# Three input chunks accumulated while the features arrive, and the rotation's two products taken from PSUM

## The chip, the cores and the metric

The kernel runs on one core of one Trainium2 chip. The metric is the device time of the core in microseconds (us); the kernel before takes 868.41 us (median of three runs, 867.76 to 868.47). The engines are called PE (matrix products), DVE (vector), ACT (scalar), POOL (GpSimd) and SP (it issues most DMAs). Products accumulate in banks of PSUM; all other tiles lie in SBUF.

## The reference

Two layers of an encoder over 16 meta tokens and 512 real ones, 1024 features, all in float32. Cut to what matters here:

```python
def hybrid_layer(x, norm_g, w_in, q_norm_g, k_norm_g, ...):
    h = rms_norm(x, norm_g)
    proj = einsum('bld,de->ble', h, w_in)
    qa, ka, va, za, qb, kb, vb, zb, ga, gb = split_cols(proj)
    qa = apply_axial_rope(rms_norm(qa.reshape(b, l, 8, 64), q_norm_g), cos, sin)
    ka = apply_axial_rope(rms_norm(ka.reshape(b, l, 2, 64), k_norm_g), cos, sin)
    oa = gqa_attention(qa, ka, va) * silu(za)             # 8 query heads, 2 key heads
    ob = neighbourhood_attention(qb, kb, vb, rpb) * silu(zb)
    mixed = sigmoid(ga) * (oa @ w_o_attn) + sigmoid(gb) * (ob @ w_o_na)
    return x + mixed @ w_out

def apply_axial_rope(x, cos, sin):
    rot = concat([-xr[16:], xr[:16], -xc[16:], xc[:16]])  # xr, xc: the 32 features for row and column
    return x * cos + rot * sin
```

## The kernel before

**Layout.** Features lie on the 128 partitions, tokens along the free axis: 528 tokens, in layer 0 as two spans of 264 (0 and 264), in layer 1 as one of 512. The input projection is made in chunks of 128 output columns: QA to QA+3 (0 to 3, the eight query heads), KA (4), VA (5), then the chunks of the two attentions and the gates. A chunk's span is 24 products into one bank: 8 feature tiles k, and for each the three products wh·hh, wh·hl, wl·hh, since weights and features are split into a high part (hi, cast by ACT) and the rest (lo, subtracted by POOL for weights at L227, by DVE for features at L324). Products go through two banks with the tag "pp" (`product`, L300); the next span takes the bank that the span before last left.

**Norm.** The features enter the products scaled by the gain alone. The squares of the input are made by ACT (L330), added by DVE (L401), split, and averaged by ten tiny products ms (L356). For Q and K each head has its own norm: ACT makes the squares of each chunk twice (qh rounded, qs full), DVE subtracts them to ql (L463), and PE averages them with four products mh for each chunk (L444).

**The head of layer 0.** Ten warming products of two instructions each come first. `piece` loads a quarter of a chunk (two feature tiles' weights), `half` the other half, `feature` a feature tile; `in_order` holds them in the order of the list. QA and QA+1 accumulate while the tiles arrive, QA in the two banks of pp, QA+1 in the two-bank score tile S (one buffer in the whole kernel); their 96 products are written out at L423. QA+2, QA+3, KA, VA follow through `product`.

**Q and K.** `rotated` empties a chunk: ACT reads a bank three times (q times gain L459, squares L460 and L461), after which the bank is free. `rotate` then works in SBUF on DVE: shuffle of q by 16 partitions (L468), times sin (L469), q times cos (L470), their sum (L471). `stack_pair` splits q for the score products (ACT L481, DVE L483) and moves halves by DMA.

**Order.** Every engine runs its instructions in the order that the scheduler put them in when the program was built; `issue_after` holds one behind another in it. The attentions run beside the projections: `product` calls `tick()` behind each span, and the two `Side` objects put their parts (score products S, softmax, transposes pt, value products av) at set numbers of ticks: GQA_AT and NA_AT for the units, NORM_AT for the norms ("tokens" for split, ms and spread; "squares" for mh). S and the one for meta queries, Sm, share the single two-bank buffer, which DVE's L750 empties.

## Time and profile before

| | us |
|---|---|
| median of three runs | 868.41 (867.76 to 868.47) |
| the profiled execution's own time | 869.61 |
| its span, from the first to the last instruction | 867.8 |
| PE busy in the span | 854.8 |
| DVE, ACT, POOL busy in the span | 537.2, 494.2, 365.6 |
| first product of QA+3 / of KA / of VA | 27.70 / 35.34 / 41.75 |

A row of the timeline gives the start, the busy time, the engine, the line and operation, out<-in, shapes, and in brackets how long the engine had stood idle and who released it. A row of the groups gives the count, the busy time, the mean of one in ns and the idle time before. A row of the waits gives who waits for whom, the us in total, how often, and the longest. A row of windows gives, for a stretch, its length and each engine's busy time with its count, the granted clock of PE (1.00 is full speed), the DMA share and GB/s.

### The profile page before, as it was taken

How to read it: one execution, taken by the hardware profiler on the slowest of the kernel's cores; microseconds unless marked ns; L12 is line 12 of the kernel's file. 1: busy time of each engine (PE TensorE's matmuls, PEld its weight loads, DVE VectorE, ACT ScalarE, POOL GpSimd, SP SyncE). 2: the span in 40 equal slices, each digit the busy share in tenths (PEclk: the TensorE clock that was granted, in tenths of full speed). 3: DMA queues.
4: the chain of work that ended last, by engine and by line, in shares of the span. 5: the costliest groups of instructions: out<-in, count | busy, mean ns of one | idle time of the engine just before them, and what ended most of it. 6: DMA issues, size and time to landing. Idle time of an engine off the chain costs nothing.

```text
span 867.8 us, 16234 instructions
## 1 busy us (share of the span) xinstructions
PE 854.8 (99%) x5976; PEld 790.6 (91%) x5976; DVE 537.2 (62%) x1277; ACT 494.2 (57%) x1170; POOL 365.6 (42%) x300
## 2 busy tenths in 40 slices
PE   8999999999999999999999999999999999999997
PEld 8999999999999999999998989898988888888786
DVE  5985667676774574436547656677767646454633
ACT  7645677677774555333445456677767645543432
POOL 5564323443223332544764643334333333334751
PEclk9999999999999999999999999999999999999999
DMA  6364253325112222325555664235422222223602
GB/s 223 99 186 145 93 150 99 106 73 153 49 50 75 62 67 81 98 86 152 148 139 127 171 198 130 79 95 151 145 81 73 86 73 73 87 85 97 206 25 97
DMA packets 64671, 95.76 MB, mean 110 GB/s; under 512 B 22864, under 2 KB 23376, under 8 KB 64592
## 3 DMA queue, kind: packets, MB, share of 16 engines
q1 hardware_dynamic: 63872, 93.66, 36.8%
q8 instruction: 47, 0.77, 0.4%
q10 hardware_dynamic: 720, 1.06, 0.3%
q14 instruction: 32, 0.26, 0.1%
HBM read 76.72 MB, written 4.19 MB: 93 GB/s over the span
## 4 chain that ended last, share of the span: by engine, by line
PE 86%; ACT 6%; DVE 4%; DMA 2%; issue 1%; POOL 0%; SPq 0%; POOLq 0%; ACTq 0%; DVEq 0%
PE pp L311 18%; PE pp L309 18%; PE pp L310 17%; PE y L309 4%; PE y L311 4%; PE y L310 3%; PE av L797 3%; PE pt L124 3%; PE avb L940 2%; PE pf L1115 2%; PE S L525 2%; PE pf L1117 2%; PE pf L1116 1%; PE S L526 1%; DMA x<-in_xT_dram 1%
## 5 line engine op out<-in xcount | busy, mean ns | idle before, releaser
L227 POOL TENSOR_TENSOR wlo<-raw,whi 128x512 fp32r<-128x512 f32 x214 | 285.3, 1337 | 425.4 <-ACT whi L226 341.7
L309 PE MATMUL pp<-hh,whi 128*128 128x264 f32 (+1 forms) x1056 | 334.7, 317 | 0.6 <-ACT qs L461 0.5
L311 PE MATMUL pp<-hh,wlo 128*128 128x264 f32 (+1 forms) x1056 | 329.3, 312 | 0.0
L310 PE MATMUL pp<-hl,whi 128*128 128x264 f32 (+1 forms) x1056 | 328.6, 311 | 0.0
L226 ACT CAST whi<-raw 128x512 fp32r<-128x512 f32 x214 | 131.5, 619 | 152.7 <-PE pp L310 58.3
L311 PEld LDWEIGHTS pp<-hh,wlo 128*128 128x128 f32 x1056 | 198.8, 188 | 10.7
L309 PEld LDWEIGHTS pp<-hh,whi 128*128 128x128 f32 x1056 | 198.6, 188 | 10.1 <-ACT qs L461 1.1
L310 PEld LDWEIGHTS pp<-hl,whi 128*128 128x128 f32 x1056 | 199.3, 189 | 9.0
L750 DVE CUSTOM_DVE_ANT_1 P<-S,r 128x528 f32<-128x528 f32 x64 | 45.1, 704 | 18.5 <-PE S L526 17.6
L183 DVE TENSOR_TENSOR ptl<-pt,pth 128x512 fp32r<-128x512 f32 x64 | 44.0, 689 | 18.0 <-ACT pth L182 17.2
L1012 DVE TENSOR_TENSOR mg<-pp,rbc 128x264 f32<-128x264 f32 (+1 forms) x48 | 24.8, 517 | 43.2 <-PE pp L311 42.7
L754 ACT ACTIVATE P<-P,st 128x528 f32<-128x528 f32 x64 | 47.2, 737 | 1.9
L876 ACT ACTIVATE Pb<-Pb,stb 128x208 f32<-128x208 f32 (+1 forms) x64 | 31.1, 487 | 16.6 <-DVE stb L874 16.3
L124 PE MATMUL pt<-ident,P 128*128 128x128 f32 x256 | 39.3, 275 | 0.6 <-DVE ptl L183 0.4
L182 ACT CAST pth<-pt 128x512 fp32r<-128x512 f32 x64 | 37.2, 583 | 4.2 <-PE pt L124 2.9
L1013 ACT ACTIVATE mg<-mg 128x264 f32<-128x264 f32 (+1 forms) x48 | 23.7, 494 | 24.4 <-DVE mg L1012 24.4
L310 PE MATMUL pp<-mx,whi 128*128 128x264 f32 x128 | 36.6, 286 | 0.0
L309 PE MATMUL pp<-mx,whi 128*128 128x264 f32 x128 | 36.4, 285 | 0.0
L311 PE MATMUL pp<-mx,wlo 128*128 128x264 f32 x128 | 36.3, 284 | 0.0
L797 PE MATMUL av<-pth,VA 128*128 128x256 f32 x128 | 35.0, 296 | 0.0
L756 DVE TENSOR_SCALAR P<-P,st 128x528 f32<-128x528 f32 x64 | 33.7, 527 | 2.1
L797 PE MATMUL av<-ptl,VA 128*128 128x256 f32 x128 | 33.1, 281 | 0.0
(526 smaller groups left out, 1764.3 us busy)
## 6 DMA issues: line engine op xcount, KB each, us to landing
raw<-in_w_dram SPq DMA_DIRECT2D x214, 256.0 KB, 2.7
bias<-in_bias_dram SPq DMA_DIRECT2D x16, 480.0 KB, 4.5
KB<-KB SPq DMA_DIRECT2D x24, 280.0 KB, 4.0
rawl<-in_w_dram SPq DMA_DIRECT2D x16, 256.0 KB, 2.9
x<-in_xT_dram SPq DMA_DIRECT2D x8, 264.0 KB, 6.3
xr<-in_xT_dram SPq DMA_DIRECT2D x8, 264.0 KB, 3.9
Q<-q SPq DMA_DIRECT2D x16, 128.0 KB, 2.9
x1d<-xt SPq DMA_DIRECT2D x32, 64.0 KB, 2.8
```

The source lines that it names most:

```text
L124: nc.tensor.transpose(ps, src, ident[:n, :n])
L182: split_at["hi"] = nc.scalar.copy(hi, src)
L183: split_at["any"] = nc.vector.tensor_sub(lo, src, hi.bitcast(F32))
L226: cast = nc.scalar.copy(hi, raw)
L227: sub = nc.gpsimd.tensor_sub(lo, raw, hi.bitcast(F32))
L309: nc.tensor.matmul(ps, wh, rh[:, a:b], start=i == 0, stop=False)
L310: nc.tensor.matmul(ps, wh, rl[:, a:b], start=False, stop=False)
L311: nc.tensor.matmul(ps, wl, rh[:, a:b], start=False, stop=i == n - 1)
L750: newest["max"] = nc.vector.tensor_tensor_reduce(p[:n].rearrange("p (i k) -> p i k", i=2), S[:n, :, :HALF], scale[:n].unsqueeze(2).to_broa ...
L754: nc.scalar.activation(p[:n], p[:n], AF.Exp, bias=st[:n, 1:2], scale=1.0, accum_out=st[:n, 2:3])
L756: nc.vector.tensor_scalar_mul(p[:n], p[:n], st[:n, 3:4])
L797: nc.tensor.matmul(c["av"], rows2(c["t"][i][0]), c["t"][i][1], start=i == 0, stop=i == 8)
```

## The change

- Seven warming products instead of ten.
- The first stage accumulates three chunks, QA to QA+2 (144 products), QA+2 in the two banks avn and avg of the value products. Weights come by row tiles: for each k one transfer of 128 x 384 (the three chunks' weights for that k), ahead of feature tile k; the first is issued by ACT's queue. hh of k = 0 is made in halves. The three products of a tile stand in the order wh·hh, wl·hh, wh·hl.
- The squares of the input and their adds stand among the features (k - 3 behind k); those of tiles 6 and 7 come with the emptying of QA and QA+1.
- Q and K are emptied by two engines: ACT makes the two squares, DVE takes bank · gain · cos to q and bank · gain · sin to a new tile "turned" (`qt`), which is shuffled and added to q. The sign of sin moves to the other side of the shuffle. The two multiplies in SBUF and ACT's scaled read are gone. Issue hints chain DVE's products from PSUM to each other, and ACT's squares to each other.
- NORM_AT of layer 0 and the tick of `meta_columns` are other numbers, and QA+2 no longer goes through `product`, so it ticks no side work.

```diff
-NORM_AT = ({"tokens": (1, 4, 6), "squares": (2, 2, 2, 3, 2), "heads": (2, 3, 5, 7, 6), "values": (1, 4)},
+NORM_AT = ({"tokens": (1, 2, 4), "squares": (1, 1, 2, 3, 2), "heads": (2, 3, 5, 7, 6), "values": (1, 4)},
...
-    sign = np.where(np.arange(HD) % 32 < 16, -1.0, 1.0).astype(np.float32)[:, None]
+    sign = np.where(np.arange(HD) % 32 < 16, 1.0, -1.0).astype(np.float32)[:, None]
...
-        for _ in range(10):
+        for _ in range(7):
             nc.tensor.matmul(warm[:, :P], zero, zero, start=True, stop=True)
+    w3 = w[0, QA:QA + 3].rearrange("c p n -> (c p n)").rearrange("(k p n) -> k p n", k=KT, p=P)
+    raw3 = {0: slot("K", "rawp0")[:, :3 * P]}
+    nc.scalar.dma_start(raw3[0], w3[0])
...
-            order = order[1:2] + order[3:]
+            order = order[6:]
...
-    def normed(l, k, x, n):
+    def normed(l, k, x, n, spans=None):
...
-        h_last["hi"] = nc.scalar.mul(hi[:, :n], x, g_in[l][:, k:k + 1])
+        for a, b in spans or ((0, n),):
+            h_last["hi"] = nc.scalar.mul(hi[:, a:b], x[:, a:b], g_in[l][:, k:k + 1])
...
+    def row_tile(k):
+        if k not in raw3:
+            raw3[k] = slot("K" if k < 4 else "E", f"rawp{k}")[:, :3 * P]
+            in_turn(raw3[k], w3[k])
+        hi, lo = (slot("O", f"w{'hl'[v]}p{k}", F32R)[:, :3 * P] for v in range(2))
+        done[0] = nc.scalar.copy(hi, raw3[k]).ins
+        done[1] = nc.gpsimd.tensor_sub(lo, raw3[k], hi.bitcast(F32)).ins
+        pieces[k] = hi, lo
...
+    def add_up(k):
+        sq = square(k)
+        if k == 0:
+            total["ss"] = sq
+        else:
             nc.vector.tensor_add(total["ss"], total["ss"], sq)
...
+    for k in range(KT):
+        in_order(lambda: row_tile(k))
+        in_order(lambda: feature(k))
+        if k > 2:
+            in_order(lambda: add_up(k - 3))
+    in_order(lambda: add_up(5))
+    in_order(next_weights)
...
+    def first_products(c, k):
+        wh, wl = (t[:, P * (c - QA):P * (c - QA + 1)] for t in pieces[k])
+        for wt, rt in ((wh, 0), (wl, 0), (wh, 1)):
             for ps, a, b in first[c]:
                 nc.tensor.matmul(ps, wt, h[k][rt][:, a:b], start=k == 0 and wt is wh and rt == 0,
-                                 stop=k == KT - 1 and wt is wl)
+                                 stop=k == KT - 1 and rt == 1)
+    for k in range(4):
+        for c in range(QA, QA + 3):
+            first_products(c, k)
+    for c, k in ((0, 4), (1, 4), (0, 5), (1, 5), (0, 6), (2, 4), (0, 7), (1, 6), (1, 7), (2, 5), (2, 6), (2, 7)):
+        first_products(QA + c, k)
...
             for ps, a, b in project(c, full):
-                nc.scalar.mul(q[:, a:b], ps, g)
-                nc.scalar.activation(qh[:, a:b], ps, AF.Square)
-                evac["last"] = nc.scalar.activation(sq[:, a:b], ps, AF.Square)
-            with tc.high_priority():
+                with ExitStack() as held:
+                    if "last" in evac:
+                        held.enter_context(tc.issue_after(evac["last"].ins))
+                    nc.scalar.activation(qh[:, a:b], ps, AF.Square)
+                    evac["last"] = nc.scalar.activation(sq[:, a:b], ps, AF.Square)
+                for t, table in ((q, cos), (turned, sin)):
+                    with tc.high_priority(), ExitStack() as held:
+                        if "turn" in evac:
+                            held.enter_context(tc.issue_after(evac["turn"].ins))
+                        evac["turn"] = nc.vector.scalar_tensor_tensor(t[:, a:b], ps, g, table[:, a:b], op0=ALU.mult, op1=ALU.mult)
+            with tc.high_priority(), tc.issue_after(evac["turn"].ins):
                 evac["low"] = nc.vector.tensor_sub(ql[:, :n], sq[:, :n], qh[:, :n].bitcast(F32))
...
-                nc.vector.stream_shuffle(sh[:, :n], q[:, :n], [(i + 16) % 32 for i in range(32)])
-                nc.vector.tensor_mul(sh[:, :n], sh[:, :n], sin[:, :n])
-                nc.vector.tensor_mul(q[:, :n], q[:, :n], cos[:, :n])
+                nc.vector.stream_shuffle(sh[:, :n], turned[:, :n], [(i + 16) % 32 for i in range(32)])
                 nc.vector.tensor_add(q[:, :n], q[:, :n], sh[:, :n])
...
-                    side_gqa.later(5, meta_columns)
+                    side_gqa.later(4, meta_columns)
```

The order on DVE around the emptying of QA+2 and QA+3, before (names: q is the chunk, its number behind it; qr the shuffled copy, qs and qh the two squares, Q the rounded half for the scores):

```order
L463 TENSOR_TENSOR ql_2_385<-qs_2_383,qh_2_384 128x528
L471 TENSOR_TENSOR q_0_345<-q_0_345,qr_0_372 128x528
L470 TENSOR_TENSOR q_1_360<-q_1_360,cos_338 128x528
L468 STREAM_SHUFFLE qr_2_467<-q_2_382 128x528
L471 TENSOR_TENSOR q_1_360<-q_1_360,qr_1_377 128x528
L469 TENSOR_TENSOR qr_2_467<-qr_2_467,sin_339 128x528
L470 TENSOR_TENSOR q_2_382<-q_2_382,cos_338 128x528
L483 TENSOR_TENSOR q_0_345<-q_0_345,Q_0_472 128x512
```

And of the change, at the same place (qt is the turned tile; pp_3_0 and pp_3_264 are the two banks of QA+3):

```order
L485 SCALAR_TENSOR_TENSOR q_2_438<-pp_2_avg,gains,cos_391 128x264
L485 SCALAR_TENSOR_TENSOR qt_2_442<-pp_2_avg,gains,sin_392 128x264
L487 TENSOR_TENSOR ql_2_441<-qs_2_439,qh_2_440 128x528
L493 TENSOR_TENSOR q_1_415<-q_1_415,qr_1_435 128x528
L492 STREAM_SHUFFLE qr_2_452<-qt_2_442 128x528
L505 TENSOR_TENSOR q_0_398<-q_0_398,Q_0_455 128x512
L485 SCALAR_TENSOR_TENSOR q_3_461<-pp_3_0_484,gains,cos_391 128x264
L485 SCALAR_TENSOR_TENSOR qt_3_465<-pp_3_0_484,gains,sin_392 128x264
L485 SCALAR_TENSOR_TENSOR q_3_461<-pp_3_264_525,gains,cos_391 128x264
L485 SCALAR_TENSOR_TENSOR qt_3_465<-pp_3_264_525,gains,sin_392 128x264
```

DVE now reads the banks themselves, in its own order between other work; no row of it read them before.

The order on PE between QA+3 and KA, before (ssh and ssl are the split squares of the input; of ten ms products the last two are shown):

```order
L356 MATMUL ms_550<-means_r,ssh_426 128x2
L356 MATMUL ms_550<-means_r,ssl_427 128x2
L444 MATMUL mh_342<-qh_2_384,means_r 10x264
L444 MATMUL mh_342<-ql_2_385,means_r 10x264
L309 MATMUL pp_4_0_597<-hh_0_137,whi_4_0_484 128x264
L310 MATMUL pp_4_0_597<-hl_0_138,whi_4_0_484 128x264
```

And of the change:

```order
L459 MATMUL mh_395<-qh_2_440,means_r 10x264
L459 MATMUL mh_395<-ql_2_441,means_r 10x264
L459 MATMUL mh_395<-qh_3_463,means_r 10x264
L361 MATMUL ms_554<-means_r,ssh_517 128x2
L313 MATMUL pp_4_0_600<-hh_0_134,whi_4_0_474 128x264
L314 MATMUL pp_4_0_600<-hl_0_135,whi_4_0_474 128x264
```

One ms product is left in front of KA, the other nine stand within KA's first span; the first mean product of QA+3 has come forward.

The order on PE at the end of chunk 37 of layer 0, before (S_4_1_1 stands some 70 rows above; y is the product of the output weights):

```order
L311 MATMUL pp_37_264_3920<-hh_7_205,wlo_37_1_3727 128x264
L124 MATMUL pt_4_1_2_3947<-ident,P_4_1_3697 128x128 x4
L525 MATMUL Sm_1_0_3958<-KA0h_1110,Q2m_1027 64x264
L526 MATMUL Sm_1_0_3958<-KA0l_1111,Q2m_1027 64x264
L309 MATMUL y_46_0_3976<-ob_0_2000,whi_46_0_3864 128x264
```

And of the change, from the last score products of S_4_1_1, which stand behind chunk 37's last product:

```order
L547 MATMUL S_4_1_1_3920<-KA0h_1104,Q_2_675 128x264
L548 MATMUL S_4_1_1_3920<-KA0l_1105,Q_2_675 128x264
L818 MATMUL av_4_0_3882<-pth_4_0_2_3763,VA_764 128x256
L818 MATMUL av_4_0_3882<-ptl_4_0_2_3764,VA_764 128x256
L818 MATMUL av_4_0_3882<-pth_4_0_2_3763,VA_764 128x256
L818 MATMUL av_4_0_3882<-ptl_4_0_2_3764,VA_764 128x256
L818 MATMUL av_4_0_3882<-ga_119,VA_764 128x256
L124 MATMUL pt_4_1_0_3962<-ident,P_4_1_3767 128x128
L124 MATMUL pt_4_1_2_3985<-ident,P_4_1_3767 128x128
L547 MATMUL Sm_1_0_3996<-KA0h_1104,Q2m_1018 64x264
L548 MATMUL Sm_1_0_3996<-KA0l_1105,Q2m_1018 64x264
```

S_4_1_1 has moved from ahead of chunk 37 to behind it, and Sm_1_0 has stayed.

More of the change, by code (lines that the diff above doesn't have):

```diff
@@ L371, in in_order @@
             part()
-    def piece(c, i):
-        raw = slot("K", f"rawp{c}_{i}")[:, :2 * P]
-        hi, lo = (slot("O", f"w{'hl'[v]}p{c}_{i}", F32R)[:, :2 * P] for v in range(2))
-        nc.sync.dma_start(raw, w[0, c][:, 2 * P * i:2 * P * (i + 1)])
-        done[0] = nc.scalar.copy(hi, raw).ins
-        done[1] = nc.gpsimd.tensor_sub(lo, raw, hi.bitcast(F32)).ins
-        pieces[c, i] = hi, lo
-    def half(c):
-        weights(0, c, 1, 1)
-        done[:] = split_at["weights"]
+    def row_tile(k):
[6 more added lines that the diff above has]
+        pieces[k] = hi, lo
     def feature(k):
@@ L387, in feature @@
             xs.extend(two("M", f"x0_{k}"))
-        nc.sync.dma_start(xs[k], xT[k])
-        h.append(normed(0, k, xs[k], NTOK))
+        in_turn(xs[k], xT[k])
+        h.append(normed(0, k, xs[k], NTOK, ((0, HALF), (HALF, NTOK)) if k == 0 else None))
         done[0] = h_last["hi"].ins
-    for part in ((piece, QA, 0), (feature, 0), (piece, QA + 1, 0), (feature, 1), (piece, QA, 1), (piece, QA + 1, 1),
-                 (feature, 2), (feature, 3), (half, QA), (feature, 4), (half, QA + 1), (feature, 5), (feature, 6), (feature, 7)):
-        in_order(lambda: part[0](*part[1:]))
@@ L396, in input_squares @@
-    def input_squares(ks):
-        return [squared(k == 0, xs[k], NTOK, f"0_{k}") for k in ks]
-    def sum_up(sqs):
-        for sq in sqs:
-            nc.vector.tensor_add(total["ss"], total["ss"], sq)
-    total, late = {}, []
-    with tc.issue_after(h_last["hi"].ins), tc.issue_after(h_last["lo"].ins):
-        total["ss"], *sqs = input_squares(range(3))
-        sum_up(sqs)
-    with tc.issue_after(h_last["square"].ins):
-        weights(0, QA + 2, 1, 1)
-    with tc.issue_after(split_at["weights"][0]):
-        sum_up(input_squares((3, 4)))
-        late.append(input_squares((5, 6)))
+    total = {}
@@ new lines, in square, with next_weights @@
+    def square(k):
+        sq = squared(k == 0, xs[k], NTOK, f"0_{k}")
+        done[0] = h_last["square"].ins
+        return sq
+    def add_up(k):
[3 more added lines that the diff above has]
+        else:
+            nc.vector.tensor_add(total["ss"], total["ss"], sq)
+    def next_weights():
+        weights(0, QA + 3, 0, 1)
+        done[:] = split_at["weights"]
+    for k in range(KT):
[3 more added lines that the diff above has]
+            in_order(lambda: add_up(k - 3))
@@ L414, in trunk_kernel @@
+    in_order(lambda: add_up(5))
+    in_order(next_weights)
     first, ends = {}, ((0, HALF), (HALF, NTOK))
+    two_banks = ps_s.tile([P, 2, 512], F32, tag="S", name=f"pp0_{QA + 1}")
     for c, ps in ((QA, [bank(ps_p, f"pp0_{QA}_{a}", "pp")[:, :HALF] for a, _ in ends]),
-                  (QA + 1, ps_s.tile([P, 2, 512], F32, tag="S", name=f"pp0_{QA + 1}"))):
-        first[c] = [(ps[i] if c == QA else ps[:, i, :HALF], a, b) for i, (a, b) in enumerate(ends)]
-    for c, k in sorted(((c, k) for c in first for k in range(KT)), key=lambda x: (x[1] + 2 * (x[0] > QA and x[1] > 3), x[0])):
-        wh, wl = (t[:, P * (k % 4):P * (k % 4 + 1)] for t in weights(0, c, k // 4, 1)) if k > 3 else (
-            t[:, P * (k % 2):P * (k % 2 + 1)] for t in pieces[c, k // 2])
-        for wt, rt in ((wh, 0), (wh, 1), (wl, 0)):
+                  (QA + 1, [two_banks[:, i, :HALF] for i in range(2)]),
+                  (QA + 2, [bank(ps_a, f"pp0_{QA + 2}_{tag}", tag)[:, :HALF] for tag in ("avn", "avg")])):
+        first[c] = [(ps[i], a, b) for i, (a, b) in enumerate(ends)]
@@ L457, in rotated @@
             qh, ql = slot("G", f"{name}h{l}_{c}", F32R), slot("G", f"{name}l{l}_{c}", F32R)
+            turned = slot("K", f"{name}t{l}_{c}")
             for ps, a, b in project(c, full):
-                nc.scalar.mul(q[:, a:b], ps, g)
-                nc.scalar.activation(qh[:, a:b], ps, AF.Square)
-                evac["last"] = nc.scalar.activation(sq[:, a:b], ps, AF.Square)
-            with tc.high_priority():
+                with ExitStack() as held:
[9 more added lines that the diff above has]
+            with tc.high_priority(), tc.issue_after(evac["turn"].ins):
                 evac["low"] = nc.vector.tensor_sub(ql[:, :n], sq[:, :n], qh[:, :n].bitcast(F32))
@@ L566, in trunk_kernel @@
                 if l == 0 and j < 2:
-                    sum_up(late[j])
+                    with tc.issue_after(evac["last"].ins):
+                        add_up(6 + j)
                 if l == 0 and j == 0:
                     turn = rotate
-                    with tc.issue_after(evac["last"].ins):
-                        late.append(input_squares((7,)))
                 else:
@@ L1161 @@
     w = np.concatenate([wi, wa, wb, wo], axis=1).reshape(DEPTH, NCHUNK, P, KT * P)
+    w[0, QA:QA + 3] = w_in[0][:, :3 * P].reshape(3, P, KT * P)
     w[DEPTH - 1, WOUT:] = w_out[DEPTH - 1].reshape(KT, P, D)
```

## The prediction

> **What bounds the kernel now.** Three views in this order. The page first: how busy each engine is, and which engines make up the chain that ended last.

> ```profile
> PE 854.8 (99%) x5976; PEld 790.6 (91%) x5976; DVE 537.2 (62%) x1277; ACT 494.2 (57%) x1170; POOL 365.6 (42%) x300
> PE 86%; ACT 6%; DVE 4%; DMA 2%; issue 1%; POOL 0%; SPq 0%; POOLq 0%; ACTq 0%; DVEq 0%
> ```

> TensorE is the bound; only shorter or fewer waits of PE, or fewer products, can shorten the run. Then the waits of PE, once for the first 60 us, once for 60 to 440 (the rest of layer 0), and the busy time in the stretch where layer 1 makes its Q and K.

> ```profile
> PE pp L423 <- DVE hl L324: 1.3, 3, 0.7
> PE warm L132 <- DVE one L138: 1.0, 1, 1.0
> PE pp L309 <- ACT qs L461: 0.5, 1, 0.5
> ...
> PE S L526 <- DVE KA0l L516: 0.5, 1, 0.5
> PE pt L124 <- DVE ptl L183: 0.4, 2, 0.2
> PE vtd L676 <- DVE na L730: 0.3, 1, 0.3
> ...
> 440.00:460.00 20.00, 20.00 (x123) 17.73 (x122) 9.86 (x15) 9.29 (x16) 11.40 (x9) 1.00 0.53 123
> 460.00:480.00 20.00, 20.00 (x125) 17.51 (x124) 15.29 (x23) 11.01 (x23) 9.34 (x7) 1.00 0.55 137
> 480.00:500.00 20.00, 20.00 (x147) 18.45 (x146) 12.67 (x36) 10.12 (x20) 12.30 (x9) 1.00 0.65 175
> ```

> So the waits are 2.8 us in the head and 1.8 in the rest of layer 0 (six rows, the last three of 0.2 each not shown); in layer 1's Q and K stage PE is busy 20.00 of 20.00 three times over, so what ACT and DVE save there is worth nothing, and a later release of a bank is covered. I price layer 1 at 0. If the cover were gone (DVE has 15.29 of 20 there), it would cost, not gain: 0 to 1 us.

> The head is where the time can move. Its steps on PE:

> ```profile
> 1.04 4.64 PE L132 MATMUL warm<-zero 128*128 128x128 f32 x20 [1.04 <-DVE one L138]
> 5.33 0.76 PE L423 MATMUL pp<-hh,whp 128*128 128x264 f32 x2
> 5.91 0.42 PE L423 MATMUL pp<-hl,whp 128*128 128x264 f32 x2
> 6.17 0.41 PE L423 MATMUL pp<-hh,wlp 128*128 128x264 f32 x2
> ...
> 26.74 0.28 PE L444 MATMUL mh<-qh,means_r 128*10 128x264 f32 x1
> ...
> 27.70 0.28 PE L309 MATMUL pp<-hh,whi 128*128 128x264 f32 x1
> 27.82 0.28 PE L310 MATMUL pp<-hl,whi 128*128 128x264 f32 x1
> 27.94 0.28 PE L311 MATMUL pp<-hh,wlo 128*128 128x264 f32 x1
> ...
> 33.59 0.25 PE L356 MATMUL ms<-means_r,ssl 128*128 128x2 f32 x1
> 33.70 0.25 PE L356 MATMUL ms<-means_r,ssh 128*128 128x2 f32 x1
> ...
> 35.34 0.39 PE L309 MATMUL pp<-hh,whi 128*128 128x264 f32 x1
> ```

> Products of 264 columns follow each other every 0.121 us. QA to QA+2 are done at 26.74, QA+3 starts at 27.70 behind eight mean products (8 x 0.12), KA at 35.34. Up to KA's start I compare the two kernels; that is the first term.

> **Term 1a, the first stage.** Three warming products of two instructions each go: from 1.04 to 5.33 there are 20, 0.21 each, so 1.3 us; the halved hh0 then sets the start, near 4.8. 24 products for each of six spans, 144 x 0.121 = 17.4, would end at 22.2 without a wait. But the tiles come in more slowly:

> ```profile
> 5.00:10.00 5.00, 4.67 (x32) 4.15 (x31) 2.25 (x3) 2.18 (x5) 2.72 (x3) 1.00 0.94 303
> 10.00:15.00 5.00, 4.21 (x29) 3.58 (x29) 3.26 (x3) 4.68 (x8) 3.02 (x2) 1.00 0.99 370
> ...
> 12.89 2.16 ACT L323 ACTIVATE hh<-x,gains 128x528 fp32r<-128x528 f32 x3
> ...
> 13.66 2.85 DVE L324 SCALAR_TENSOR_TENSOR hl<-x,gains,hh 128x528 fp32r<-128x528 f32 x3 [0.22 <-ACT hh L323]
> ```

> Ahead of hh7, 8 x (264 + 192) = 3648 KB must land where 3136 KB did: 512 KB at 370 GB/s is 1.4 us, so hh7 ends at 15.05 + 1.4 = 16.4 (the DMA share of 0.99 leaves no room). Each feature brings 456 KB, 1.23 us, but DVE now does an hl and an add of squares for each: 0.95 (2.85 / 3) + 0.93 (L401 below) = 1.9. It falls behind from k = 4, whose hh ends at 16.4 - 3.7 = 12.7: four hl and three adds, 4 x 0.95 + 3 x 0.93 = 6.6, end at 19.3 with hl7. Bounds: 17.2 (hh7, then an hl alone, 0.8) and 21.0 (seven operations at 0.62 and all four of POOL's subtractions in the way at 1.0 each). By the program's order 32 products remain after hl7's first use: 19.3 + 3.9 = **23.2** (22.2 to 24.9) against 26.74. PE gains 3.5 us here.

> **Term 1b, what PE meets then.** Behind 48 products of QA+3 (5.8) and 14 small ones (1.7) PE is ready for KA at 30.7. KA's first half takes the bank of QA+3's first half, which ACT alone released before and which now also waits for two products on DVE. So DVE's list between hl7 and that release counts (the order on DVE is fixed by the chain of issue hints): two adds of squares, 12 products from PSUM, three ql, two more adds, three shuffles, two rotation adds, one subtraction of the stacking, and the two products that release the bank.

> ```profile
> L401 DVE TENSOR_TENSOR sq<-sq,sq 128x528 f32<-128x528 f32 x7 | 6.5, 930 | 0.6 <-ACT sq L330 0.3
> L469 DVE TENSOR_TENSOR qr<-qr,sin 128x528 f32<-128x528 f32 x4 | 6.0, 1498 | 0.0
> L470 DVE TENSOR_TENSOR q<-q,cos 128x528 f32<-128x528 f32 x4 | 5.0, 1246 | 0.0
> L468 DVE STREAM_SHUFFLE qr<-q 128x528 f32<-128x528 f32 x4 | 2.9, 761 | 0.0
> L1002 DVE SCALAR_TENSOR_TENSOR qb<-pp,rbc 128x264 f32<-128x264 f32 x1 | 0.4, 433 | 1.9 <-PE pp L311 1.9
> ...
> 26.68 1.72 DVE L469 TENSOR_TENSOR qr<-qr,sin 128x528 f32<-128x528 f32 x1
> 28.33 1.80 DVE L470 TENSOR_TENSOR q<-q,cos 128x528 f32<-128x528 f32 x1
> 32.99 0.69 DVE L471 TENSOR_TENSOR q<-q,qr 128x528 f32<-128x528 f32 x1
> 33.61 0.69 DVE L470 TENSOR_TENSOR q<-q,cos 128x528 f32<-128x528 f32 x1
> 48.26 0.42 DVE L664 TENSOR_TENSOR va<-pp,rbc 128x264 f32<-128x264 f32 x1
> 48.60 1.46 DVE L470 TENSOR_TENSOR k<-k,cos 128x528 f32<-128x528 f32 x1
> ...
> 25.08 4.48 POOL L227 TENSOR_TENSOR wlo<-raw,whi 128x512 fp32r<-128x512 f32 x3 [4.28 <-ACT whi L226]
> 44.78 6.43 POOL L227 TENSOR_TENSOR wlo<-raw,whi 128x512 fp32r<-128x512 f32 x4
> ```

> A DVE operation on two tiles in SBUF takes 0.69 and starts 0.62 after the last (32.99, 33.61); beside POOL's subtraction it takes 1.7 to 1.8 (26.68, 28.33), so a meeting costs 1.1. One that reads PSUM takes 0.42 in the middle of POOL's row (48.26 within 44.78 to 51.2): no meeting. The new operation has the form of L1002, 0.43 long; the next start is 0.34 later (48.60), I take 0.36. Ten two-tile operations 6.2, three shuffles at 0.66 2.0, 14 products from PSUM 5.0: 13.2, from 19.3 to 32.5. Before, the eight multiplies of the two groups took 11.0 where 8 x 0.69 = 5.5 would do: five meetings in eight. Now POOL's order has six subtractions beside the ten operations; since shuffles and products from PSUM lie between them, I take four meetings, 4.4 (0 to 6.6). ACT and DVE both read QA+1's two-bank tile and wait for each other's reads: two reads of ACT at about 0.4, 0.8 (0 to 1.6). The release comes at 37.7, KA at **37.8** against 35.34: 2.5 later, though PE was done sooner; PE waits some 7 us, part of it already at the mean products of ql_2. Nine tiny ms products are still owed, 0.11 each (33.59, 33.70), one mean product is ahead: +0.9. **Head: +3.4 us**, from -1.8 (no meetings, KA at 32.6) to +7.

> The rotation's own saving, two multiplies of 1.4 mean for each chunk, is in this sum: four products of 0.36 in their place, and one read of ACT. It is real, but on DVE the products stand in front of the release, where the old multiplies stood behind it. The tables of cos and sin are needed sooner as well: two of 264 KB behind one more half chunk, 784 KB at 370 GB/s after hh7 could begin (14.3 + 1.4), are there at 17.8; the first product from PSUM wants them at 20.5, so this costs nothing unless the transfer slips by 2.7 us.

> [...]

> **Term 2, the rest of layer 0.** QA+2 is no longer made by the loop that ticks the side work, so every attention unit stands two ticks later against the projections. The 0.5 us wait of S for KA0l goes (S comes after the next chunk). On the other side Sm_1_0 now stands right behind S_4_1_1 on the one score buffer, five value products and two transposes apart (0.8 us); the buffer is free after DVE's read:

> ```profile
> L750 DVE CUSTOM_DVE_ANT_1 P<-S,r 128x528 f32<-128x528 f32 x64 | 45.1, 704 | 18.5 <-PE S L526 17.6
> ```

> 0.70 at the least, and DVE stands idle for S in only 23 of 64 cases, so mostly an operation of up to 0.7 runs first: +1.0 (0.1 to 2). For the other units, which stand beside new neighbours, the trace gives no row: the old alignment lost 1.8 us in all, and the units feed on DVE's results; I take +2.5 (0 to +4.5). Sum of term 2: **+3.0** (-0.5 to +6).

> **Sum.** 3.4 + 3.0 + 0 = +6.4: span 867.8 to 874.2; around it lie 1.8 us (869.61 - 867.8), which gives 876.0 for the profiled run. That run lay 1.2 above the median of 868.41, so the forecast median is **874.8**.

> **Rivals.** (a) Faster: POOL's subtractions fall where DVE runs shuffles and PSUM products, so no meeting; KA starts at 32.6 and the shift costs nothing: -1.8 - 0.5, **866.1**. For it: DVE waits for nobody but hl7; against it: two rows of 1.7 and more in a row at 26.68 and 28.33, with POOL as loaded after. It turns at two meetings. (b) No change: two meetings and a shift that gives and takes alike, head +0.9, shift -0.5, **868.8**. (c) The tiles don't follow: hl7 at 21.0 and six meetings: the list ends at 21.0 + 13.2 + 6.6 + 0.8 = 41.6, head +7, shift +3, **878.4**. [...]

> **How the numbers follow.** Forecast 0.58, (a) 0.15, (b) 0.13, (c) 0.09, (d) 0.05. A measurement of this kernel tells about 0.2% (1.7 us) from no change. Faster: (a), 0.15; same: (b), 0.13; slower: the rest, 0.72. The forecast's own range is 870.5 to 879.5. The range of 8 in 10 leaves half of (a) below 866.5 and, above 880.0, a third of (c) and the tail of the forecast.

> **What would show it.** QA+3's first product at 23 to 25; hl7's end near 19.3; a wait of PE on DVE's products from PSUM (L485) of several us ahead of KA, and one at the mean products; those products at 0.42 to 0.45 beside POOL, the adds at 1.7; KA at 36 to 40; PE busy throughout at 440 to 500; Sm waiting for L750's read of the score buffer. Wrong, if KA starts before 35 or if the waits of PE in 60 to 440 stay under 2 us.

## The result, and the profile after

The change makes the kernel slower: 879.62 us (median of four runs, 879.03 to 879.91) against 868.44 us, a ratio of 1.0127 with a 95% interval of 1.0111 to 1.0142, or 11.2 us. The forecast was 874.8 with a range from 866.5 to 880.0; direction and range held, but the forecast missed two fifths of the loss.

The waits of PE come first, for the first 60 us and for 60 to 450 (who waits for whom; us in total, times, longest).

```profile
PE pp L313 <- DVE qt L485: 3.1, 1, 3.1
PE pp L432 <- ACT hh L328: 1.6, 1, 1.6
PE mh L459 <- DVE ql L487: 1.3, 1, 1.3
PE warm L132 <- DVE one L142: 1.0, 1, 1.0
PE mh L459 <- DVE qt L485: 0.6, 1, 0.6
...
PE Sm L547 <- DVE st L771: 1.5, 1, 1.5
PE vtd L697 <- DVE na L751: 0.9, 3, 0.4
PE pt L124 <- DVE VB L187: 0.6, 1, 0.6
```

The wait of KA for DVE's product from PSUM (qt, L485) is there with 3.1 us, the one at the mean products with 1.3, Sm behind S with 1.5. But these waits, and the 1.6 us that the first product waits for hh, don't explain how late the head ends. PE's timeline in the head shows it (start, busy time, operation, and in brackets the idle time before it):

```profile
6.03 0.81 PE L432 MATMUL pp<-hh,whp 128*128 128x264 f32 x2 [1.64 <-ACT hh L328]
...
25.49 0.28 PE L313 MATMUL pp<-hh,whi 128*128 128x264 f32 x1
...
38.42 0.59 PE L313 MATMUL pp<-hh,whi 128*128 128x264 f32 x1 [3.09 <-DVE qt L485]
38.81 0.42 PE L314 MATMUL pp<-hl,whi 128*128 128x264 f32 x1
39.03 0.42 PE L315 MATMUL pp<-hh,wlo 128*128 128x264 f32 x1
...
49.47 0.28 PE L315 MATMUL pp<-hh,wlo 128*128 128x264 f32 x1
49.59 0.38 PE L569 MATMUL rb<-ident,rx 128*128 128x128 f32 x2
```

QA+3 starts at 25.49 (before 27.70), KA at 38.42 (before 35.34). Behind KA's start the products are 0.22 apart instead of 0.12. The windows show the cause in the column before the last two, the clock granted to PE:

```profile
35.00:40.00 5.00, 1.91 (x11) 1.78 (x10) 5.00 (x10) 1.07 (x3) 0.76 (x1) 0.75 0.52 157
40.00:45.00 5.00, 5.00 (x25) 5.00 (x25) 2.00 (x6) 0.00 (x0) 1.36 (x1) 0.50 0.11 26
45.00:50.00 5.00, 5.00 (x33) 5.00 (x33) 1.93 (x4) 1.58 (x4) 1.79 (x5) 0.73 0.23 52
```

Behind the waits PE runs at half clock until about 47.8: in 40 to 45 it is busy all the time and does 25 products where before, in the same stretch, it did 44. "Busy" alone doesn't tell the two apart; the granted clock and the distance between rows do.

So the 10.3 us of the two profiles (span 878.1 against 867.8, where before's stands 1.2 above its median) divide as follows, by the same products in both. KA starts 3.1 late (38.42 - 35.34). From there to the norm's spread (rb, before at 41.29, now at 49.59) the same 48 products of KA take 11.17 instead of 5.95; nine tiny products that now stand among them are worth 1.0 at full clock (0.11 each before, at 33.59 and 33.70), the other **4.2 us** are the half clock. At rb the change is 8.3 late, at the first product of layer 0's output projection 10.3 (411.70 against 401.37): 2.0 for the shifted units. At the last product it is still 10.3: layer 1 gives nothing, as PE is busy there throughout:

```profile
440.00:460.00 20.00, 20.00 (x161) 19.80 (x161) 9.53 (x14) 8.91 (x15) 14.81 (x11) 1.00 0.54 136
460.00:480.00 20.00, 20.00 (x98) 16.24 (x97) 11.69 (x20) 8.38 (x16) 10.21 (x8) 1.00 0.49 119
```

### The profile page after: what moved, and what is told of

Same layout as the page of the kernel before. It is cut to its first block, busy times and chain, and to the rows that moved or that the text cites. A ratio compares the mean times of both kernels' runs of the same rounds, so it can differ in the third digit from the quotient of the medians.

```text
span 878.1 us, 16229 instructions
## 1 busy us (share of the span) xinstructions
PE 858.0 (98%) x5970; PEld 794.9 (91%) x5970; DVE 529.7 (60%) x1289; ACT 487.4 (55%) x1155; POOL 365.1 (42%) x300
## 3 DMA queue, kind: packets, MB, share of 16 engines
q1 hardware_dynamic: 63728, 93.46, 36.5%
## 4 chain that ended last, share of the span: by engine, by line
PE 89%; ACT 4%; DVE 4%; issue 1%; DMA 1%; POOL 0%; POOLq 0%; ACTq 0%; DVEq 0%
PE pp L313 18%; PE pp L315 18%; PE pp L314 18%; PE y L313 3%; PE y L315 3%; PE y L314 3%; PE av L818 3%; PE pt L124 3%; PE avb L961 2%; PE pf L1136 2%; PE S L547 2%; PE pf L1138 2%; PE pf L1137 1%; PE S L548 1%; PE pp L432 1%
## 5 line engine op out<-in xcount | busy, mean ns | idle before, releaser
L231 POOL TENSOR_TENSOR wlo<-raw,whi 128x512 fp32r<-128x512 f32 x210 | 278.3, 1328 | 427.0 <-ACT whi L230 324.1
L313 PE MATMUL pp<-hh,whi 128*128 128x264 f32 (+1 forms) x1040 | 331.1, 318 | 3.5 <-DVE qt L485 3.1
L230 ACT CAST whi<-raw 128x512 fp32r<-128x512 f32 x210 | 128.9, 618 | 160.4 <-PE pp L314 61.2
L313 PEld LDWEIGHTS pp<-hh,whi 128*128 128x128 f32 x1040 | 197.2, 190 | 12.7 <-DVE qt L485 3.2
L771 DVE CUSTOM_DVE_ANT_1 P<-S,r 128x528 f32<-128x528 f32 x64 | 45.1, 705 | 18.4 <-PE S L548 17.5
L187 DVE TENSOR_TENSOR ptl<-pt,pth 128x512 fp32r<-128x512 f32 x64 | 44.1, 690 | 17.2 <-ACT pth L186 16.3
L1033 DVE TENSOR_TENSOR mg<-pp,rbc 128x264 f32<-128x264 f32 (+1 forms) x48 | 24.7, 518 | 41.8 <-PE pp L315 41.6
L124 PE MATMUL pt<-ident,P 128*128 128x128 f32 x256 | 39.8, 275 | 0.9 <-DVE VB L187 0.6
L314 PE MATMUL pp<-mx,whi 128*128 128x264 f32 x128 | 36.5, 286 | 0.0
```

The source lines that it names most:

```text
L124: nc.tensor.transpose(ps, src, ident[:n, :n])
L187: split_at["any"] = nc.vector.tensor_sub(lo, src, hi.bitcast(F32))
L230: cast = nc.scalar.copy(hi, raw)
L231: sub = nc.gpsimd.tensor_sub(lo, raw, hi.bitcast(F32))
L313: nc.tensor.matmul(ps, wh, rh[:, a:b], start=i == 0, stop=False)
L314: nc.tensor.matmul(ps, wh, rl[:, a:b], start=False, stop=False)
```

## The experiments

The theory after the result: (1) DVE's products from PSUM free QA+3's bank too late for KA; (2) the pauses that this makes bring the half clock; (3) the units that stand two ticks later cost in the rest of layer 0. Rivals: the three-chunk stage itself is the loss; the half speed has another cause; the later loss only follows from the late head. All runs in one table (median; ratio to before with its interval; clock, lowest to highest of the runs' means; the profiled run's start of KA; and how much later than in the profile of before rb and the output projection come):

| run | us | ratio (95%) | clock | KA | rb | output |
|---|---|---|---|---|---|---|
| the change | 879.62 | 1.0127 (1.0111 to 1.0142) | 0.992 to 0.994 | 38.4 | +8.3 | +10.3 |
| e1 new first stage, old emptying | 874.14 | 1.0060 (1.0040 to 1.0079) | 0.994 to 0.999 | 33.0 | -0.3 | +1.9 |
| e2 old first stage, new emptying | 872.76 | 1.0052 (1.0036 to 1.0068) | 0.995 to 0.998 | 40.6 | +5.1 | +3.9 |
| e4 old places of the units | 876.78 | 1.0100 (1.0083 to 1.0117) | 0.992 to 0.996 | 38.0 | +5.3 | +3.9 |
| e5 16 useless products | 876.86 | 1.0098 (1.0083 to 1.0113) | 0.997 to 0.999 | 38.1 | +6.0 | +8.0 |
| e6 ten warming products | 879.08 | 1.0123 (1.0105 to 1.0141) | 0.993 to 0.995 | 38.1 | +7.3 | +9.3 |
| e3 KA in other banks | 875.78 | 1.0086 (1.0068 to 1.0104) | 0.996 | 33.0 | +2.4 | +5.9 |
| c1 e1 and e4 | 872.08 | 1.0041 (1.0029 to 1.0054) | 0.995 to 0.997 | 34.0 | +3.8 | +2.8 |
| c2 c1 and ten warming products | 871.45 | 1.0036 (1.0023 to 1.0048) | 0.995 to 0.997 | 33.1 | +2.9 | +2.2 |
| e7 58 useless products | 877.45 | 1.0098 (1.0081 to 1.0114) | 0.998 | 40.8 | +5.5 | +7.5 |
| e8 bank freed first | 873.53 | 1.0061 (1.0038 to 1.0084) | 0.992 to 0.999 | 35.4 | +1.9 | +3.8 |
| c5 e3, e4, e8, ten warming | 869.25 | 1.0005 (0.9996 to 1.0014) | 0.997 to 0.999 | 32.9 | -0.4 | -1.1 |
| c6 c5, mean products later | 869.48 | 1.0008 (0.9999 to 1.0017) | 0.998 to 0.999 | 31.4 | -0.4 | -1.1 |

**The two halves of the change.** e1 takes `rotated` and the sign of sin from the kernel before; e2 puts the new `rotated` into the kernel before.

```diff
 # e1, in the change
+                nc.scalar.mul(q[:, a:b], ps, g)
                 nc.scalar.activation(qh[:, a:b], ps, AF.Square)
...
-                for t, table in ((q, cos), (turned, sin)):
...
-                        evac["turn"] = nc.vector.scalar_tensor_tensor(t[:, a:b], ps, g, table[:, a:b], op0=ALU.mult, op1=ALU.mult)
...
+                nc.vector.tensor_mul(sh[:, :n], sh[:, :n], sin[:, :n])
+                nc.vector.tensor_mul(q[:, :n], q[:, :n], cos[:, :n])
...
 # e2: the same lines the other way round, in the kernel before
```

> The new first stage with the old emptying of Q and K (ACT reads a bank three times and frees it, the two multiplies stay in SBUF on DVE). If the wait for DVE's products from PSUM, and the half clock behind it, make the loss of the head: KA starts at 34 to 36 with no pause of PE over 1.5 us, the granted clock stays at 1.00 from 35 to 50, and the time is about 871.5 (3 us over before: 2 from the shift of the units by two ticks, 1 from the mean products still owed). If the three-chunk stage itself is the cause (tiles that come too slowly): 877 to 880.

> The old first stage and its ticks with the new emptying (two products from PSUM on DVE). If the release by DVE is what costs: KA at 39 to 41 instead of 35.3, waits of PE on L471's successor line of 1.5 to 2 us each, time 873 to 875, and 876 or more if a pause grows long enough to bring the half clock back. If the first stage alone is the cause: 867 to 869.

With the old emptying KA starts at 33.0 and, in the profiled run, which keeps its clock, the head is level with before at rb (-0.3): at full clock the three-chunk stage isn't the loss, but it isn't a gain either (c1 and c2 below show what it costs where the clock falls). The profiled run (871.36, clock 0.999) is where it was expected; the median isn't, since three of the five runs have a lower clock (0.997 and twice 0.994) and take 874.1 to 875.5. The new emptying on the old first stage starts KA at 40.6 and is 5.1 late at rb, near what was expected (872.8 for 873 to 875); its waits are longer than expected for one row, 2.2 us for the squares of the input. Part of it is half clock again, 0.66 in 30 to 35:

```profile
PE pp L309 <- ACT sq L330: 2.2, 1, 2.2
PE pp L309 <- DVE qt L470: 1.5, 1, 1.5
...
30.00:35.00 5.00, 3.25 (x15) 3.17 (x16) 5.00 (x11) 1.37 (x4) 0.38 (x1) 0.66 0.44 123
```

**The bank that KA waits for.** e3 gives KA the two banks that QA+2 leaves; e8 keeps the banks and puts DVE's rotation of QA+1 and QA+2 and the first stacking behind QA+3's emptying.

```diff
 # e3
...
-            ps = bank(ps_p, f"{name}{l}_{c}_{a}", "pp")[:, :b - a]
+            ps = (bank(ps_a, f"{name}{l}_{c}_{a}", tags[a > 0]) if tags else bank(ps_p, f"{name}{l}_{c}_{a}", "pp"))[:, :b - a]
...
-            return first[c] if l == 0 and c in first else product(l, c, h, full)
+            return first[c] if l == 0 and c in first else product(l, c, h, full, tags=("avn", "avg") if l == 0 and c == KA else ())
 # e8
...
+                if l == 0:
+                    turns.append(rotate)
+                    while turns and j in (1, 3) and (j == 3 or len(turns) > 1):
+                        turns.pop(0)()
...
+            if l == 0 and j == 3:
+                stack_pair(0)
+                stack_pair(1)
```

> The changed kernel with KA's two spans put into the two banks that QA+2 leaves (avn, avg), so that KA need not wait for DVE's reading of QA+3. If the wait for that release is the main loss and the half clock its consequence: KA starts at 33 to 34.5, no wait of PE over 2 us, and the time is 3.5 to 6 us less, 873.5 to 876. If DVE's list is what everything waits for anyway: the waits reappear behind KA (at the products for the norm and at VA's bank), and the time is 877 to 879.

> The changed kernel with the rotation of QA+1 and QA+2 and the first two subtractions of the stacking put behind QA+3's emptying, so that DVE frees QA+3's first bank earlier; nothing is left out. If the place of DVE's products from PSUM behind that list is what delays KA: KA starts at 35 to 36.5 instead of 38.4, the 3.1 us wait falls under 1.2, and the time is 2 us less at the same clock, up to 5 less if the clock returns sooner: 874.5 to 877.5. If the list's total length counts, wherever it stands: KA earlier but the waits behind it longer, 879 to 880.

Both start KA sooner, at 33.0 and 35.4, and both win: 3.8 us (875.78) and 6.1 us (873.53, more than expected). In e3 the waits reappear behind KA, at the norm's products, and half clock with them (0.86 and 0.80 in 40 to 50). So its first expectation came true in every number (KA at 33.0, no wait over 1.7, 875.78), and of the second the place of the waits, but not the time.

```profile
PE ms L361 <- DVE ssl L187: 1.7, 1, 1.7
PE pp L432 <- ACT hh L328: 1.5, 1, 1.5
PE rb L569 <- POOL rx L197: 1.1, 1, 1.1
```

In e8, which leaves nothing out and only moves DVE's work, the longest wait is 1.9 (expected under 1.2) and the profiled run keeps its clock at 1.00 from 30 to 40. So its gain is 3.0 us at KA's start and the rest the clock, and it isn't had in every run: one of the four takes 877.22 at a mean clock of 0.992. Where DVE's products stand in its list decides, not its length.

**The clock.** e5 puts 16 products into an unused bank in front of KA; e7, with ten warming products, puts 58 of them where PE waits from 28 to 41 (6 and 12 behind QA+3's spans, 40 in front of KA). The lines are those of e5.

```diff
+    def keep_busy(n):
+        busy = bank(ps_t, "busy", "tp")
+        with tc.high_priority(), tc.issue_after(ended["mm"].ins):
+            for _ in range(n):
+                nc.tensor.matmul(busy[:, :HALF], h[0][0][:, :P], h[0][0][:, :HALF], start=True, stop=True)
...
+        if l == 0:
+            keep_busy(16)
         k, rotate = rotated(KA, g_k[l], True, "k")
```

> The changed kernel with sixteen products of 264 columns into an unused bank put in front of KA, so that PE works through most of its wait; nothing else is removed. If the half speed of KA (products 0.22 apart, granted clock 0.5 from 40 to 45) comes from PE's pause: KA still starts near 38.4, its products are 0.12 apart, clock 1.00, and the time is 3 to 4 us below the change, 875.6 to 876.6. If the half speed has another cause (DVE and ACT reading PSUM beside it): KA stays slow and the time is that of the change or 0.5 more.

> The changed kernel with ten warming products and 58 products of 264 columns into an unused bank (7 us of useless work): 6 behind QA+3's first span, 12 behind its second, 40 in front of KA, so that PE never waits between 20 and 41 us. KA starts later than in the run with ten warming products alone (at about 41 instead of 38.4), with the nine tiny products already done. If pauses of PE bring the half clock: granted clock 1.00 in every stretch, every run at 0.998 or more, and 875.5 to 877, 2 to 3.5 us under that run in spite of the added work. If the half speed has another cause: 881 to 884.

In e5 KA starts at 38.09 and first runs at 0.12; waits of 1.1 and 0.4 us are left around its start, and then the clock falls all the same, from 40.4 to 43.8, 3.4 us long. So the expectation of a full clock wasn't met. The two runs with a mean clock of 0.997 take 877.6, the two with 0.999 take 876.0 and 876.1. In e7, with 7 us of work that nobody needs, every window from 5 to 50 us has the full clock (the longest wait left behind 20 us is 0.6), all four runs are at 0.998, and the time is 2.2 us under the change and 1.6 under e6 (a little over what was expected):

```profile
35.00:40.00 5.00, 5.00 (x45) 5.00 (x43) 5.00 (x10) 0.90 (x2) 0.58 (x1) 1.00 0.59 162
40.00:45.00 5.00, 5.00 (x44) 5.00 (x43) 3.07 (x8) 0.67 (x2) 1.74 (x5) 1.00 0.31 71
45.00:50.00 5.00, 5.00 (x44) 5.00 (x43) 2.52 (x7) 3.40 (x8) 2.56 (x2) 1.00 0.24 60
```

KA starts 2.4 us later there than in the change, and still rb comes 2.8 sooner (46.75 against 49.59). That shows the cause: it is PE's pauses, not DVE and ACT reading PSUM beside it, since these do the same here.

**The start.** e6 has ten warming products again, for the first products stood 0.22 apart from 6.03 to about 10.

> The changed kernel with ten warming products again. If the slow start matters (in the change's profile the first products stood 0.22 apart from 6.03 to about 10, before only until 5.91): the clock is full from about 6, the first stage ends 0.5 to 1 us sooner, and the time is 1 to 2 us less, 877.6 to 878.6. If DVE's list sets the end of the head in any case: 879.0 to 879.8, with KA's start unchanged near 38.4.

The first stage runs at full speed from the start then (37 products in 5 to 10 us where the change has 18), but KA starts at 38.1 for 38.4 and the time is 879.08 for 879.62: DVE's list sets the end of the head, so most of the gain is waited away.

**The places of the units.** e4 moves the starting ticks of the side work by two.

```diff
-GQA_AT_TICK, NA_AT_TICK = (0, 0), (1, 1)
+GQA_AT_TICK, NA_AT_TICK = (2, 0), (3, 1)
```

> The changed kernel with the side work's starting ticks moved by two, so that the attention units stand at the same places of the projections as before. If the shift costs what the marks of the traces say (8.3 us late at the norm's spread, 10.3 late at the end of layer 0): 2 to 3 us less than the change, 876.6 to 877.6, and the wait of Sm (1.5 us) gone. If the later loss comes from the late head alone and not from the places: 879.6.

The run is 2.8 us under the change (876.78), the wait of Sm is gone, and between rb and the output projection it loses nothing (+5.3, then +3.9), where the change loses 2.0 more. That its rb is 3.0 sooner than the change's comes from the clock rather than the places: the profiled run is the fastest of the four (873.49; the others take 876.6 to 877.6) and has half clock for 3.4 us only, 38.1 to 41.5. The other runs agree: every one with the shifted places loses 2.0 to 3.5 us on that way (in e3, with 3.5, a stretch of half clock from 43.6 to 47.0 lies behind rb), every one with the old places gains 0.6 to 1.4 against the profile of before, which itself stands 1.2 above its median. So the later loss is that of the places, not of the late head.

**Together.** c1 is e1 with e4, c2 has ten warming products as well, c5 is the change with e3, e4, e8 and ten warming products, and c6 the same with "squares" at (2, 2, 2, 3, 2).

> The new first stage with the old emptying, and the side work's starting ticks moved by two. Both found parts undone: the 3 us of the shift come off the run with the new first stage and old emptying (871.4 to 875.5 there): 868.5 to 871. If the three-chunk stage were worth anything by itself, it would have to come under 868.3 here.

> The same with ten warming products. If the early clock decides over the first stage: 0.5 to 1.5 us under the run with seven, and a smaller spread between runs; it could reach 867.5 to 869. If not: the same as with seven.

> All mends at once on the changed kernel: ten warming products, QA+3 released first, KA in the banks of QA+2, the side work's places as before. If the three causes found are all there is, the head is within 1 us of before's and nothing is lost later: 867.5 to 869.5 with the clock full, 870 to 871.5 where the small pauses left (some 2 us) still bring one stretch of half clock. If something else is lost: 872 or more.

> The run with all mends, with the mean products of QA and QA+1 one tick later (squares 2, 2, 2, 3, 2 as before), so that PE doesn't wait 1.3 us for them between QA+3's two spans but does them behind both. If that wait is real loss: 0.5 to 1 us less, 868.0 to 869.0, level with before or 0.3 us under it, with a ratio between 0.9985 and 1.0005. If the wait only moves behind QA+3: 869.2 as there, and one half-clock stretch (870 to 871) where the moved wait adds to KA's.

c1 and c2 stay over before, by 3.6 and 3.1 us in the ratio's terms, and over the times that were expected; only that c2 is 0.6 us under c1 and spreads less came out as written. So the rival isn't wholly away: the three-chunk stage by itself, with the old emptying and the old places, costs 3 us and more. Their profiles (c1's rows below) show waits of PE of 1.6 to 1.8 us in all between 20 and 60, none over 0.7, and yet a half clock of about seven us in 35 to 45.

```profile
PE ms L361 <- DVE ssl L187: 0.7, 1, 0.7
PE pp L313 <- ACT qs L476: 0.6, 1, 0.6
PE mh L459 <- ACT qh L475: 0.3, 1, 0.3
...
35.00:40.00 5.00, 4.30 (x24) 4.09 (x24) 3.82 (x8) 1.14 (x2) 3.32 (x3) 0.69 0.45 129
40.00:45.00 5.00, 5.00 (x29) 5.00 (x29) 3.36 (x7) 1.66 (x4) 1.10 (x5) 0.63 0.47 108
```

c5 mends the causes named above and is level with the kernel before, 869.25 with a ratio of 1.0005 (0.9996 to 1.0014): together the mends take the whole loss away, and nothing of a gain is left. c6's wait only moved (1.0 us at ql in place of 1.3 at qt); it is no better. No version here beats the kernel before.

## Why the prediction was right, and where its size was off

**Term 1a, the first stage:** hl7's end is right (19.2 for 19.3; its row is the first of those below), its consequence isn't. The first product came at 6.03, not 4.8, since the first weights were there only at 4.8 (ACT's cast follows at 4.81), and the first products ran at half speed (0.22 apart from 6.03 to about 10, 0.12 behind that). So PE was behind the tiles, and QA+3 started at 25.49 instead of 23.2. It cost little, because DVE's list decided: e6, where QA+3 starts at 24.35, has KA only 0.4 sooner.

**Term 1b, DVE's list:** right in sum. The second product from QA+3's first span ends at 38.37, forecast 37.7, and KA follows at 38.42, forecast 37.8. PE waited 5.0 us on the way (0.6, 1.3 and 3.1), forecast some 7. The parts differ, and that their errors nearly cancel is luck. DVE's rows:

```profile
17.94 1.25 DVE L329 SCALAR_TENSOR_TENSOR hl<-x,gains,hh 128x528 fp32r<-128x528 f32 x1 [0.20 <-ACT hh L328]
19.11 2.42 DVE L406 TENSOR_TENSOR sq<-sq,sq 128x528 f32<-128x528 f32 x2
22.62 0.49 DVE L485 SCALAR_TENSOR_TENSOR q<-pp,gains,cos 128x264 f32<-128x264 f32 x1 [1.09 <-ACT qs L479]
23.03 0.48 DVE L485 SCALAR_TENSOR_TENSOR qt<-pp,gains,sin 128x264 f32<-128x264 f32 x1
24.23 1.74 DVE L487 TENSOR_TENSOR ql<-qs,qh 128x528 fp32r<-128x528 f32 x1
28.14 0.49 DVE L485 SCALAR_TENSOR_TENSOR q<-pp,gains,cos 128x264 f32<-128x264 f32 x1 [0.74 <-ACT qs L479]
33.71 0.92 DVE L487 TENSOR_TENSOR ql<-qs,qh 128x528 fp32r<-128x528 f32 x1
34.55 1.78 DVE L493 TENSOR_TENSOR q<-q,qr 128x528 f32<-128x528 f32 x1
37.89 0.48 DVE L485 SCALAR_TENSOR_TENSOR qt<-pp,gains,sin 128x264 f32<-128x264 f32 x1
```

A product from PSUM starts 0.40 after the last, not 0.36 (14 of them: 0.6). DVE waited 1.8 for ACT's reads (1.09 and 0.74), not 0.8; of the 1.09 the first 0.4 pass before ACT itself can start, at 21.91, since PE is late with QA. The meetings with POOL cost 3.5 in place of 4.4: one each at 19.11, 24.23 and 34.55, part of one at 33.71. The new products meet nobody (0.48 beside POOL's rows too).

**The step that failed is the clock:** the sum put it at nothing, and among the rivals only (d), with a chance of 0.05, was the half clock. Before's trace shows none to price it from: its granted clock is 1.00 in every window of 0.1 us from 0 to 75. The half clock isn't an alternative to the long wait but its consequence, and it cost 4.2 us. Term 1b itself forecast that PE would wait some 7 us. In the change 10.2 us at half clock came with three waits of 0.6, 1.3 and 3.1 in ten us, and in c1 6.8 us with three of 0.3 to 0.7.

**Term 2, the shift:** forecast +3.0, of it 1.0 for Sm and 0.5 gained at KA0l. Measured +2.0 on the way from rb to the output projection, 1.5 of it at Sm, and 2.8 between the medians of the change and of e4. Against the runs with the old places, which stand 0.6 to 1.4 lower on that way, it is 2.6 to 3.4, so the size was right. The waits of PE in 60 to 450 came to 4.2 us, before to 1.8. KA0l's wait is gone, as said.

**Layer 1:** 0, as said (10.3 late at its start and at its end).

In sum: 3.1 + 1.0 (owed products, forecast 0.9) + 4.2 + 2.0 = 10.3, against 3.4 + 3.0. By this sum the loss without the clock would have been 6.1, near the 6.4 that was forecast.

## What to carry to other kernels

Where a step moves the reading of a bank to another engine, count what stands ahead of it in that engine's order: KA waited 3.1 us here for the last reader of its bank (L485), and moving other work behind it won 6 us without saving an instruction, about half of it the earlier start of KA and half the clock. Where the matrix engine comes to wait at all in a stretch that had no waits, price the half clock behind it as a chance, not the wait alone: eight of the profiles here have 3.4 to 10.2 us of it, those of e1, e7, e8 and c5 none up to 50 us. And where side work is timed by counted steps, leaving steps out moves all of it; put the counter back before judging the rest.

## What the runs showed of the hardware

The half clock came behind short waits, and not in every run: e1 and c1 have the same three waits around KA's start (0.3, 0.6 and 0.7 us), and e1's profiled run keeps 1.00 while c1's falls to 0.69 in 35 to 40 and 0.63 in 40 to 45.

```profile
34.10:37.50 3.40, 0.66 (x5) 1.00 0.40 142
37.50:40.90 3.40, 2.48 (x11) 0.50 0.55 131
40.90:44.30 3.40, 3.40 (x18) 0.50 0.00 0
44.30:47.70 3.40, 3.40 (x17) 0.50 0.29 67
...
33.50:36.90 3.40, 2.19 (x16) 1.00 0.47 116
36.90:40.30 3.40, 3.40 (x17) 0.50 0.37 116
40.30:43.70 3.40, 3.40 (x18) 0.50 0.64 146
```

In the step ahead of the fall PE was busy for 0.66 us in the change, but for 2.19 in c1. The busy time alone doesn't decide, for e4 keeps its clock until 38.1, behind 3.4 us with 2.05 busy (31.3 to 34.7). No wait lasted a whole step: the longest, ahead of KA, was 3.1 us (the change, e4 and e6). What brings the fall in one run and not in another isn't shown. In the change, c1, c2 and e6 the last step stays at half although PE is busy throughout the step ahead of it; in all four that step holds small mean products, two columns wide (nine from 41.45 to 43.01 in the change). Whether these matter wasn't tried by itself.

The granted-clock column reads 1.00 in 5 to 10 us in the change, though the products there are 0.22 apart; the rows' distance tells more than the column at the start. And the runs of one kernel spread by 4 us, and their mean clock is all that tells them apart on record (e1: 871.36 at 0.999, 875.51 at 0.994).
